# Modulation weights in pieces of 256 rows by 512 columns, loaded behind all of x, summed in operations of 1024 columns

## Chip, cores and metric

One core of a Trainium2 chip. The metric is the device time of one execution in microseconds (us), as the median of the runs shown. The engines are PE (TensorE: matrix products and transposes), DVE (VectorE), ACT (ScalarE), POOL (GpSimd) and SP (SyncE, which here only issues DMA transfers). They run in parallel, each in its own program order, and wait for one another by semaphores.

## The reference, cut to what the change touches

```python
def _rmsnorm(x, g):
    inv = lax.rsqrt(jnp.mean(x * x, axis=-1, keepdims=True) + EPS)
    return (x * inv) * g

def reference(x, c, w_ada, b_ada, norm_g, w_in, ...):
    mod = c @ w_ada[l] + b_ada[l]                      # 1024 -> 3 * 1024
    shift, scale, gate = jnp.split(mod, 3, axis=-1)
    h = _rmsnorm(x, norm_g[l]) * (1.0 + scale[:, None, :]) + shift[:, None, :]
    proj = h @ w_in[l]                                 # q, k, v, z of two attentions, gates
    ...                                                # attentions, gated merge, w_out, residual
    return _rmsnorm(x, final_g)
```

x is 1024 x 1024 in float32, c one row of 1024, w_ada 1024 x 3072. `shift` and `scale` are the first two thirds of `c @ w_ada`; the residual's `gate` is made later and is not touched.

## The kernel before

The program is one launch. The part that matters here is its start (`with tc.tile_pool(name="start")`, from L193), which takes x, normalises it, turns it so that the model's columns lie on the partitions, modulates it, and makes the first projections from it. The rest (further projections, two attentions, merge, output) follows and is the same text before and after.

x is held as eight tiles of 128 tokens, four in `xa` and two each in the two `xb`. The turned and normalised x is `xnT`, eight blocks k = 0 to 7 of 128 columns on the partitions by 1024 tokens. The steps of the start are functions, and the string `SEQ` (L44) sets in which order they are written, and with it the order on every engine. A word is a letter and a number: `X` loads a tile of x (L206), `L` a block of the modulation's weights (L213), `R` one of the first four blocks of w_in (L157; all three on the SP queue); `s` sums the squares of a tile on ACT (L238); `n` makes the 1/rms of four tiles, `inv`, on ACT and DVE (L245 to L247, then three small DVE steps in L188 to L190); `x` turns a tile, by scaling it on DVE (L257) and transposing it on PE (L266), or by a product with a scaled identity, `diag` (L255, L264), and copies it out of PSUM on DVE or ACT (L267).

`a` (`weigh`) forms `am`, the sum over q of c[q] times row block q of the weights, for shift and scale, with the partitions still apart: on DVE one product (L275) and seven multiply-adds onto it (L277, scalar_tensor_tensor). `f` (`factors`) sums `am` over the partitions by two small matmuls with ones into PSUM bank 1 of `pv`, which has one buffer (L288), and DVE reads them into `ashf` and `amul` (L290, L291); the next `f` waits for that reading. `m` (`modulate`) applies the two on ACT (L297) and splits the result into a high part `hhi` (a cast on ACT, L161) and a rest `hlo` (a subtraction on DVE, L162). `w` splits a block of w_in in the same way; for the four blocks of the start the subtraction runs on POOL (`POOLW`). `p` (`project`) makes three matmuls (L177 to L179) for each k and each of seven accumulators of 512 tokens: 7 x 8 x 3 = 168. The letters l and r are halves. Behind the last `p` the accumulators are evacuated (from L376) and the rest of the kernel begins.

Before, a weight block holds all 1024 rows of the columns of one k (two for k = 3 and 4): in `GROUPS` each is a block for itself, `ADATAG` names the buffer. A row of a block is 128 or 256 columns, 512 bytes or 1 KB. The first block is loaded between the first tile of x and the others.

Of the kernel before, what the change touches and what calls it, by code (L numbers as in the profile page):

```python
# [8 lines left out]
F32 = mybir.dt.float32  # L9
# [5 lines left out]
ALU = mybir.AluOpType  # L15
# [3 lines left out]
P = 128  # L19
S = 1024  # L20
D = 1024
HD = 64
KB = D // P
# [4 lines left out]
FCOL = 4096  # L28
GCOL = 4104
FP = 2  # L30
PEK = ()
EVACS = "k0 z0 g0 g1 q0 k1 q1"
PRE = 8
GACT = 1
# [4 lines left out]
POOLW = (0, 1, 2, 3)  # L39
BATCH = (4,)  # L40
CPY = "dd aa aa aa ad dd ad aa"
GROUPS = ((0,), (1,), (2,), (3, 4), (5,), (6,), (7,))
ADATAG = ("ada1", "ada1b", "ada1", "ada2", "xb1", "ada1b", "ada1")
SEQ = "X2 L0 X0 s0 X1 X3 X4 s3 a0 X7 s2 X6 X5 s1 n0 x0 L1 s4 s5 s7 s6 R0 L2 x2 f0 R2 L3 n1 x1 a3 a1 x3 x4 R1 w0 x5 f1 x7 x6 R3 m0l w1l L6 w1r m0r m1l m1r a2 w3l L5 w2 f2 a5 f3 m2 m3l a6 p0l p1l f4 p0r w3r p1r m3r f5 p2l L7 f6 m4 m5l p2r p3l p3r a7 f7 m6 m5r m7l p4 p5 p6l p6r m7r p7"  # L44
WPOOL = ()
MLAG = 2
GAHEAD = 1
# [21 lines left out]
def tile_hybrid_block(ctx, tc, x, c, w_ada, b_ada, norm_g, w_in, b_forget,  # L69
                      w_o_sb, w_o_fox, b_gate, w_out, final_g, out):  # L70
    nc = tc.nc
    x2 = x[0]
    out2 = out[0]
    wada = w_ada[0]
# [28 lines left out]
    def pv_tile(b=None):  # L103
        if b is None:
            b = bank2[0] = 1 - bank2[0]
        return ps_pv.tile([P, 512], F32, name="pv", tag="pv%d" % b)
# [6 lines left out]
    ones = const.tile([P, 1], F32, name="ones")  # L113
# [15 lines left out]
    cT = cols[:, 0:8]  # L129
# [63 lines left out]
    with tc.tile_pool(name="start", bufs=1) as sp:  # L193
# [2 lines left out]
        xt = [xa[:, t, :] for t in range(4)] + [xb[t // 2][:, t % 2, :] for t in range(4)]  # L196
        xnT = sp.tile([P, KB, S], F32, name="xnT")
        half = {"": slice(0, S), "l": slice(0, 512), "r": slice(512, S)}
        group = {k: g for g in GROUPS for k in g}
        edges = (0,) + BATCH + (TB,)  # L200
        batch = {t: b for b in range(len(edges) - 1) for t in range(edges[b], edges[b + 1])}
        adas, ams, raws, norms, sums, wsplit, bank = {}, {}, {}, {}, {}, {}, [0]
# [2 lines left out]
        def load_x(t):  # L205
            nc.sync.dma_start(xt[t], x2[t * P:(t + 1) * P, :])  # L206

        def load_ada(k):
            n = len(group[k]) * P
            tag = ADATAG[GROUPS.index(group[k])]  # L210
            ada = sp.tile([P, KB, 2, n], F32, name="ada", tag=tag, bufs=1)
            for j in range(2):
                nc.sync.dma_start(ada[:, :, j, :],  # L213
                                  wada[:, j * D + k * P: j * D + k * P + n].rearrange("(q p) n -> p q n", p=P))
            adas[k] = ada

        def load_w0(i):
            raws[i] = load_raw(wcol((QA, KA, GCOL + 8 * P, ZA)[i]), WSH)
# [47 lines left out]
                        nc.tensor.transpose(o, i, ident)  # L266
                copy(xnT[:, 4 * b:4 * b + 4, t * P:(t + 1) * P], pt.rearrange("p (a b) -> p a b", a=4))  # L267

        def weigh(k):

            n = len(group[k]) * P
            if k in PEK:
                return
            o = ams[k] = sp.tile([P, 2, n], F32, name="am", tag="am%d" % n, bufs=2)
            nc.vector.tensor_scalar(o, adas[k][:, 0], cT[:, 0:1], None, ALU.mult)  # L275
            for q in range(1, KB):
                nc.vector.scalar_tensor_tensor(o, adas[k][:, q], cT[:, q:q + 1], o, ALU.mult, ALU.add)  # L277

        def factors(k):
            k0 = group[k][0]  # L280
            pm = pv_tile(1)
            for j in range(2):
                if k in PEK:
                    for q in range(KB):
                        nc.tensor.matmul(pm[:, j:j + 1], adas[k][:, q, j, :], cT[:, q:q + 1], start=q == 0,
                                         stop=q == KB - 1)
                    continue
                nc.tensor.matmul(pm[:, j:j + 1], ams[k0][:, j, (k - k0) * P:(k - k0 + 1) * P], ones,  # L288
                                 start=True, stop=True)
            nc.vector.tensor_add(ashf[:, k:k + 1], pm[:, 0:1], b_shift[:, k:k + 1])  # L290
            nc.vector.scalar_tensor_tensor(amul[:, k:k + 1], pm[:, 1:2], b_scale1[:, k:k + 1], gT[:, k:k + 1],  # L291
                                           ALU.add, ALU.mult)
# [22 lines left out]
        def project(k, part):  # L315
            accumulators()
            for hf in {"": (0, 1), "l": (0,), "r": (1,)}[part]:
                for i in range(4):
                    if hf < len(accs[i]):
                        proj_mm(accs[i][hf], wsplit[i], hf, k, k == 0, k == KB - 1)  # L320

        todo = dict(X=load_x, L=load_ada, R=load_w0, s=square, n=norm, x=turn_x, a=weigh, f=factors, m=modulate,
                    w=split_w, p=project)
        for what in SEQ.split():
            todo[what[0]](int(what[1]), *([what[2:]] if what[0] in "mwp" else []))
# [133 lines left out]
    def largest(p):  # L459


        pt = tp_tile()
        nc.tensor.transpose(pt[0:1, :P], vmost[p], ident)
        top = at.tile([1, 1], F32, name="vtop", tag="vtop", bufs=2)
        nc.vector.tensor_reduce(top, pt[0:1, :P], mybir.AxisListType.X, ALU.max)
        nc.vector.tensor_scalar(top, top, 1e-25, None, ALU.max)
        e = top.bitcast(I32)
        nc.vector.tensor_scalar(e, e, 0x7F800000, None, ALU.bitwise_and)
        pair = vscale[p] = at.tile([1, 2], F32, name="vpow", tag="vpow", bufs=2)
        nc.vector.tensor_scalar(pair[:, 0:1].bitcast(I32), e, -1.0, float((254 + VSCALE) << 23), ALU.mult, ALU.add)  # L470
        nc.vector.tensor_scalar(pair[:, 1:2].bitcast(I32), e, 1.0, float((VSCALE + 15) << 23), ALU.mult, ALU.subtract)

    def spread(p):

        pt = tp_tile()
        nc.tensor.matmul(pt[:, 0:2], ones_row, vscale[p], start=True, stop=True)
        o = at.tile([P, 2], F32, name="vsc", tag="vsc", bufs=2)
        nc.vector.tensor_copy(o, pt[:, 0:2])
        for q in (p, p + 1):
            vscale[q], vback[q] = o[:, 0:1], o[:, 1:2]  # L480

    def sprinkle(units, marks):

        seen, marks = [0], list(marks)

        def wrap(gen):
            for _ in gen:
                seen[0] += 1
                while marks and marks[0][0] <= seen[0]:
                    marks.pop(0)[1]()  # L490
                yield 1
        for u in units:
            u.gen = wrap(u.gen)
        assert marks[-1][0] < sum(u.steps for u in units)
        return units
# [51 lines left out]
    def load_v(p):  # L547
        vraw[p] = load_raw(vd[p], [P, S], "vraw").rearrange("p (a b d) -> p a b d", a=TB, b=2)

    def take_v(p):  # L550
        raw = vraw[p]
        vv[p] = at.tile([P, TB, 2, P], F16, name="vv", tag="vv", bufs=2)
        hi, lo = vv[p][:, :, :, 0:HD], vv[p][:, :, :, HD:P]
        nc.scalar.activation(hi, raw, AF.Identity, scale=vscale[p])
        for b in range(2):
            nc.vector.scalar_tensor_tensor(lo[:, :, b], raw[:, :, b], vscale[p], hi[:, :, b], ALU.mult, ALU.subtract)
# [26 lines left out]
    def residual_gate():  # L583

        box, raw = [], {}

        def load(k):
            raw[k] = at.tile([P, D], F32, name="graw", tag="graw")
            nc.sync.dma_start(raw[k], wada[k * P:(k + 1) * P, 2 * D:3 * D])

        def weigh(k):
            if k == 0:
                box.append(at.tile([P, D], F32, name="gacc", tag="fb", bufs=2))
                box.append(at.tile([1, D], F32, name="grow", tag="fb", bufs=2))
                nc.sync.dma_start(box[1], b_ada[0:1, 2 * D:3 * D])
                nc.vector.tensor_scalar(box[0], raw[0], cT[:, 0:1], None, ALU.mult)
            else:
                nc.vector.scalar_tensor_tensor(box[0], raw[k], cT[:, k:k + 1], box[0], ALU.mult, ALU.add)

        def total(hf):  # L600
            acc, row = box
            t = slice(hf * 512, hf * 512 + 512)
            ps = tp_tile()
            nc.tensor.matmul(ps[:1], ones, acc[:, t], start=True, stop=True)
            nc.vector.tensor_add(row[:, t], ps[:1], row[:, t])
            if hf == 1:
                nc.sync.dma_start(gated, row)
        return [lambda f=f, k=k: f(k) for k in range(KB) for f in (load, weigh)] + \
               [lambda hf=hf: total(hf) for hf in range(2)]
# [411 lines left out]
    for p in range(7):  # L1021
        a, b = [], []
        if p == 0:
            g = sprinkle(gs.pop(0), [(3, lambda: largest(0)), (4, lambda: load_v(0)), (6, lambda: spread(0)),
                                     (9, lambda: take_v(0))])
# [12 lines left out]
        q = p + 1  # L1038
# [38 lines left out]
    for t in range(TB):  # L1077
# [12 lines left out]
        for i, (c0, c1) in enumerate(zip(cuts, cuts[1:])):  # L1090
            n = slice(c0, c1)
# [53 lines left out]
```

## Time and profile before

| | |
|---|---|
| median of 3 runs | 958.14 us (957.44 to 959.42) |
| the profiled execution's own time | 960.62 us |
| its span in the profile | 958.9 us |
| mean granted clock of PE | 0.983 |
| busy: PE, DVE, ACT, POOL | 901.8, 708.1, 601.9, 117.4 us |

The profile is one execution; its times are counted from the start of the span. PE's granted clock is a share of full speed: 1.00 is the level of 2.4 GHz, 0.50 that of 1.2 GHz. The start stage, to which the change is confined, lasts until about 82 us.

### The profile page before, as it was taken

The page shows a single profiled execution, that of the slowest core. Times are in us where ns is not written, and L with a number is a line of the kernel's source. Part 1 is how long each engine was busy: PE and PEld are TensorE (multiplying, and loading weights), DVE is VectorE, ACT ScalarE, POOL GpSimd, SP SyncE. Part 2 cuts the span into 40 slices and gives each one's busy share as a digit, 9 for nine tenths or more (in the row PEclk, how much of TensorE's full clock was granted, in tenths as well). Part 3 has the DMA queues.
Part 4 walks back from the last instruction along what each step waited for, and adds up shares of the span by engine and source line. Part 5 has one row for each costly group of instructions (what it writes and reads, how often), then busy time and mean ns, then how long its engine had stood idle before and what let it go on. Part 6 is the DMA issues. An engine that isn't in the chain of part 4 may idle for free.

```text
span 958.9 us, 14911 instructions
## 1 busy us (share of the span) xinstructions
PE 901.8 (94%) x5282; PEld 756.8 (79%) x5282; DVE 708.1 (74%) x1402; ACT 601.9 (63%) x1102; POOL 117.4 (12%) x191
## 2 busy tenths in 40 slices
PE   2899999999999999889999999999899998999997
PEld 2678878879878777668987888998787777788886
DVE  4984989687786788789787777657776767676544
ACT  5646777776677687678778776546656456543222
POOL 0401001000010000100001112211313011440000
PEclk9999999999999999989999999999999999899999
DMA  9943476635794562975567677958997998552221
GB/s 313 297 116 86 99 204 125 150 96 108 168 168 119 130 160 78 175 192 114 118 168 151 162 184 160 182 142 194 200 193 146 266 265 205 207 175 88 92 94 58
DMA packets 260655, 152.14 MB, mean 159 GB/s; under 512 B 157154, under 2 KB 241746, under 8 KB 260580
## 3 DMA queue, kind: packets, MB, share of 16 engines
q1 hardware_dynamic: 257588, 142.78, 60.5%
q0 software_dynamic: 2880, 8.39, 4.7%
q8 instruction: 41, 0.67, 0.3%
q14 instruction: 34, 0.28, 0.1%
q10 hardware_dynamic: 112, 0.02, 0.0%
HBM read 80.31 MB, written 24.71 MB: 110 GB/s over the span
## 4 chain that ended last, share of the span: by engine, by line
PE 45%; DVE 11%; DMA 6%; ACT 4%; issue 3%; POOL 0%; SPq 0%; DVEq 0%; ACTq 0%; POOLq 0%
PE acc L177 7%; PE acc L178 6%; PE acc L179 6%; PE z L179 4%; PE z L178 4%; PE z L177 4%; DVE pw L707 2%; DMA graw<-in_w_ada_dram 2%; PE pv L755 2%; DMA wT<-pc 2%; PE pv L756 2%; PE acc L526 2%; PE z L622 2%; PE acc L528 2%; PE z L624 2%
## 5 line engine op out<-in xcount | busy, mean ns | idle before, releaser
L177 PE MATMUL acc<-hhi,w 128*128 128x512 f32 x576 | 235.1, 408 | 13.0 <-DVE ks L377 5.4
L179 PE MATMUL acc<-hhi,w 128*128 128x512 f32 x576 | 227.6, 395 | 0.0
L178 PE MATMUL acc<-hlo,w 128*128 128x512 f32 x576 | 227.4, 395 | 0.0
L177 PEld LDWEIGHTS acc<-hhi,w 128*128 128x128 f32 x576 | 110.1, 191 | 37.2 <-issue 9.0
L725 DVE SCALAR_TENSOR_TENSOR pc<-pw,pc 128x1024 f16<-128x1024 f32 (+7 forms) x128 | 96.8, 759 | 43.3 <-ACT pc L721 42.9
L179 PEld LDWEIGHTS acc<-hhi,w 128*128 128x128 f32 x576 | 109.6, 190 | 24.1
L178 PEld LDWEIGHTS acc<-hlo,w 128*128 128x128 f32 x576 | 110.0, 191 | 19.3
L721 ACT ACTIVATE pc<-pw 128x1024 f16<-128x1024 f32 (+7 forms) x128 | 86.8, 680 | 16.3 <-DMA wT<-pc 14.7
L717 ACT ACTIVATE pw<-pw,low 128x1024 f32<-128x1024 f32 (+3 forms) x64 | 49.6, 774 | 63.0 <-DVE low L712 63.0
L765 POOL TENSOR_TENSOR ysb<-ysb,fac 128x128 f32<-128x128 f32 x64 | 34.9, 546 | 429.2 <-DVE ysb L764 283.5
L719 ACT ACTIVATE pw<-pw,low 128x1024 f32<-128x1024 f32 (+3 forms) x64 | 49.4, 772 | 47.9 <-DVE low L712 46.6
L755 PE MATMUL pv<-vv,wT 128*128 128x128 f16 x576 | 73.9, 223 | 1.7 <-DMA wT<-pc 1.7
L756 PE MATMUL pv<-vv,wT 128*128 128x128 f16 x576 | 73.7, 222 | 0.0
L526 PE MATMUL acc<-wv,hhi 128*128 128x256 f32 (+1 forms) x256 | 73.5, 287 | 0.0
L528 PE MATMUL acc<-wv,hlo 128*128 128x256 f32 (+1 forms) x256 | 72.4, 283 | 0.0
L527 PE MATMUL acc<-wv,hhi 128*128 128x256 f32 (+1 forms) x256 | 72.4, 283 | 0.0
L622 PE MATMUL z<-ks,qs 128*128 128x512 f32 (+1 forms) x192 | 66.7, 347 | 1.5 <-DVE yT L777 1.3
L700 DVE SCALAR_TENSOR_TENSOR pw<-z,pw 128x512 f32<-128x512 f32 (+4 forms) x96 | 52.8, 551 | 17.9 <-ACT pw L691 17.3
L624 PE MATMUL z<-kx,qs 128*128 128x512 f32 (+1 forms) x192 | 65.6, 342 | 0.0
L162 DVE TENSOR_TENSOR w<-wraw,w 128x1024 fp32r<-128x1024 f32 x44 | 54.0, 1228 | 12.5 <-ACT w L161 12.2
L755 PEld LDWEIGHTS <-wT 128*128 128x128 f16 x576 | 56.7, 100 | 6.9 <-issue 4.1
L707 DVE TENSOR_TENSOR_SCAN pw<-pw 128x512 f32<-128x512 f32 (+2 forms) x64 | 58.8, 919 | 1.0
(273 smaller groups left out, 2001.3 us busy)
## 6 DMA issues: line engine op xcount, KB each, us to landing
wraw<-in_w_in_dram SPq DMA_DIRECT2D x48, 512.0 KB, 5.9
gd<-stg SPq DMA_DIRECT2D x32, 256.0 KB, 3.0
kx<-ks POOLq DMA_DIRECT2D x28, 256.0 KB, 5.4
ada<-in_w_ada_dram SPq DMA_DIRECT2D x12, 512.0 KB, 8.0
graw<-in_w_ada_dram SPq DMA_DIRECT2D x8, 512.0 KB, 4.4
zd<-stg SPq DMA_DIRECT2D x16, 256.0 KB, 4.0
zt<-zd SPq DMA_DIRECT2D x32, 128.0 KB, 2.8
vraw<-vd SPq DMA_DIRECT2D x8, 512.0 KB, 3.5
```

Of the source, the lines that this page charges most:

```text
L177: nc.tensor.matmul(ps, w[0], x[0], start=first, stop=False)
L178: nc.tensor.matmul(ps, w[0], x[1], start=False, stop=False)
L179: nc.tensor.matmul(ps, w[1], x[0], start=False, stop=last)
L526: nc.tensor.matmul(ps[:, a], hhi[k][:, t], hi[:, k, :], start=k == 0, stop=False)
L528: nc.tensor.matmul(ps[:, a], hlo[k][:, t], hi[:, k, :], start=False, stop=k == KB - 1)
L622: nc.tensor.matmul(o, qs[p, j][:, tq], ks[p, j][:, s], start=True, stop=False)
L624: nc.tensor.matmul(o, qs[p, j][:, tq], kx[p, j][:, s], start=False, stop=not mask)
L707: nc.vector.tensor_tensor_scan(l[:, ::-1], l[:, ::-1], l[:, ::-1], carry[0], ALU.add, ALU.bypass)
L721: nc.scalar.activation(pair.parts(a)[0], w, AF.Copy, scale=WSCALE)
L725: nc.vector.scalar_tensor_tensor(lo, pair.logits(a), WSCALE, hi, ALU.mult, ALU.subtract)
L755: nc.tensor.matmul(y[:, a, :], w[:, b + s, :], v, start=s == 0, stop=False)
L756: nc.tensor.matmul(y[:, a, :], w[:, b + nb + s, :], v, start=False, stop=s == nb - 1)
```

## The change

The weights of shift and scale are cut otherwise. A load is now a piece of 256 rows (two row blocks q) and 512 columns (four k), for shift and for scale: 1 MB in two transfers, in runs of 2 KB. There are eight pieces, 0 to 3 for k = 0 to 3 and 4 to 7 for k = 4 to 7, in three buffers. All eight tiles of x are loaded ahead of the first piece. `weigh` of a piece makes two operations, one for each q, of 2 x 512 = 1024 columns; after four pieces `am` is whole for four k. So `factors` of k = 0 to 3 all stand behind the fourth piece, and those of k = 4 to 7 behind the eighth. `SEQ` is written anew for that. `PEK`, `GROUPS` and `ADATAG` go.

```diff
-GROUPS = ((0,), (1,), (2,), (3, 4), (5,), (6,), (7,))
-ADATAG = ("ada1", "ada1b", "ada1", "ada2", "xb1", "ada1b", "ada1")
-SEQ = "X2 L0 X0 s0 X1 X3 X4 s3 a0 X7 s2 X6 X5 s1 n0 x0 L1 s4 s5 s7 s6 R0 L2 x2 f0 R2 L3 n1 x1 a3 a1 x3 x4 R1 w0 x5 f1 x7 x6 R3 m0l w1l L6 w1r m0r m1l m1r a2 w3l L5 w2 f2 a5 f3 m2 m3l a6 p0l p1l f4 p0r w3r p1r m3r f5 p2l L7 f6 m4 m5l p2r p3l p3r a7 f7 m6 m5r m7l p4 p5 p6l p6r m7r p7"
+SEQ = "X2 X0 s0 X1 X3 X4 s3 X7 s2 X6 X5 s1 L0 L1 n0 x0 L2 s4 s5 s7 s6 a0 x2 L3 R0 n1 x1 a1 x3 x4 R1 a2 L4 w0 x5 x7 x6 a3 R2 L5 f0 m0l w1l f1 w1r m0r m1l m1r f2 R3 a4 L6 w2 f3 m2 m3l w3l p0l p1l a5 L7 p0r w3r p1r m3r p2l a6 a7 f4 f5 p2r p3l p3r f6 f7 m4 m5l m6 m5r m7l p4 p5 p6l p6r m7r p7"
...
-        def load_ada(k):
-            n = len(group[k]) * P
-            tag = ADATAG[GROUPS.index(group[k])]
-            ada = sp.tile([P, KB, 2, n], F32, name="ada", tag=tag, bufs=1)
+        def load_ada(i):
+
+            ada = adas[i] = sp.tile([P, 2, 2, 512], F32, name="ada", tag="ada", bufs=3)
+            rows_ = wada[i % 4 * 2 * P:(i % 4 + 1) * 2 * P, :]
             for j in range(2):
-                nc.sync.dma_start(ada[:, :, j, :],
-                                  wada[:, j * D + k * P: j * D + k * P + n].rearrange("(q p) n -> p q n", p=P))
-            adas[k] = ada
+                c0 = j * D + i // 4 * 512
+                nc.sync.dma_start(ada[:, :, j, :], rows_[:, c0:c0 + 512].rearrange("(q p) n -> p q n", p=P))
...
-        def weigh(k):
-
-            n = len(group[k]) * P
-            if k in PEK:
-                return
-            o = ams[k] = sp.tile([P, 2, n], F32, name="am", tag="am%d" % n, bufs=2)
-            nc.vector.tensor_scalar(o, adas[k][:, 0], cT[:, 0:1], None, ALU.mult)
-            for q in range(1, KB):
-                nc.vector.scalar_tensor_tensor(o, adas[k][:, q], cT[:, q:q + 1], o, ALU.mult, ALU.add)
+        def weigh(i):
+
+            g = i // 4
+            if i % 4 == 0:
+                ams[g] = sp.tile([P, 2, 512], F32, name="am", tag="am", bufs=2)
+            for x in range(2):
+                q = i % 4 * 2 + x
+                if q == 0:
+                    nc.vector.tensor_scalar(ams[g], adas[i][:, x], cT[:, 0:1], None, ALU.mult)
+                else:
+                    nc.vector.scalar_tensor_tensor(ams[g], adas[i][:, x], cT[:, q:q + 1], ams[g], ALU.mult, ALU.add)
...
-                nc.tensor.matmul(pm[:, j:j + 1], ams[k0][:, j, (k - k0) * P:(k - k0 + 1) * P], ones,
+                nc.tensor.matmul(pm[:, j:j + 1], ams[k // 4][:, j, k % 4 * P:(k % 4 + 1) * P], ones,
                                  start=True, stop=True)
```

How this moves instructions is shown at three places. Line numbers of the changed kernel are 2 to 3 lower than before around `load_ada` and 7 lower behind `factors`; so L274, L276 are its product and multiply-add, L281 its factors' matmul, L175 to L177 its projection.

The first place is the SP queue at the start of the program, `xa` and `xb` being x, `ada` the modulation's weights and `wraw` w_in. Before:

```order
L206 DMA xa<-in_x_dram 128x1024
L213 DMA ada<-in_w_ada_dram 128x8x128 x2
L206 DMA xa<-in_x_dram 128x1024 x3
L206 DMA xb_169<-in_x_dram 128x1024
L206 DMA xb_170<-in_x_dram 128x1024 x2
L206 DMA xb_169<-in_x_dram 128x1024
L213 DMA ada<-in_w_ada_dram 128x8x128 x2
L157 DMA wraw<-in_w_in_dram 128x8x128
```

The same queue in the changed kernel:

```order
L204 DMA xa<-in_x_dram 128x1024 x4
L204 DMA xb_169<-in_x_dram 128x1024
L204 DMA xb_170<-in_x_dram 128x1024 x2
L204 DMA xb_169<-in_x_dram 128x1024
L212 DMA ada<-in_w_ada_dram 128x2x512 x8
L155 DMA wraw<-in_w_in_dram 128x8x128 x2
```

The first block of weights has moved from the second place to behind all of x, and four pieces now stand ahead of the first block of w_in.

The second place is DVE from the scaling of the second half of x to the first `hlo`. Before:

```order
L255 TENSOR_SCALAR diag<-ident,inv 128x128
L257 TENSOR_SCALAR xb_169<-xb_169,inv 128x1024
L290 TENSOR_TENSOR ashf<-pv,cols 128x1
L291 SCALAR_TENSOR_TENSOR amul<-pv,b_scale_132,cols 128x1
L257 TENSOR_SCALAR xb_170<-xb_170,inv 128x1024
L255 TENSOR_SCALAR diag<-ident,inv 128x128
L275 TENSOR_SCALAR am<-ada,cols 128x256
L267 COPY xnT<-tp 128x4x128
L267 COPY xnT<-acc 128x4x128
L267 COPY xnT<-z 128x4x128
L162 TENSOR_TENSOR hlo<-xnT,hhi 128x512
```

In the changed kernel, from the scaling of the second `xb` (L254) to the first of four pairs that read factors (L283, L284):

```order
L254 TENSOR_SCALAR xb_170<-xb_170,inv 128x1024
L276 SCALAR_TENSOR_TENSOR am<-ada,cols,am 128x1024
L264 COPY xnT<-tp 128x4x128
L276 SCALAR_TENSOR_TENSOR am<-ada,cols,am 128x1024
L264 COPY xnT<-acc 128x4x128
L276 SCALAR_TENSOR_TENSOR am<-ada,cols,am 128x1024
L264 COPY xnT<-z 128x4x128
L252 TENSOR_SCALAR diag<-ident,inv 128x128
L276 SCALAR_TENSOR_TENSOR am<-ada,cols,am 128x1024 x2
L264 COPY xnT<-tp 128x4x128
L283 TENSOR_TENSOR ashf<-pv,cols 128x1
L284 SCALAR_TENSOR_TENSOR amul<-pv,b_scale_132,cols 128x1
```

The long weight operations now stand between the copies, and no factor is read until the last of them.

The third place is PE at the first projections; `z`, `tp` and `acc` are PSUM banks, `wqk` and `wz` split blocks of w_in. Before:

```order
L266 MATMUL tp<-ident,xb_170 128x128 x4
L177 MATMUL z<-hhi,wqk 128x512
L266 MATMUL acc<-ident,xb_170 128x128 x4
L177 MATMUL acc<-hhi,wz 128x512
L264 MATMUL z<-diag,xb_170 128x128 x4
L264 MATMUL tp<-diag,xb_170 128x128 x4
L178 MATMUL z<-hlo,wqk 128x512
```

In the changed kernel:

```order
L263 MATMUL tp<-ident,xb_170 128x128 x4
L263 MATMUL acc<-ident,xb_170 128x128 x4
L261 MATMUL z<-diag,xb_170 128x128 x4
L261 MATMUL tp<-diag,xb_170 128x128 x4
L281 MATMUL pv<-ones,am 128x1 x8
L175 MATMUL z<-hhi,wqk 128x512 x3
L175 MATMUL tp<-hhi,wqk 128x512
```

The projections no longer stand among the last transposes; the factors' eight small matmuls (four k) stand between the two.

## Rows read from the trace of the kernel before

**Rows 1.** Page, section 1: busy us (share of the span) xinstructions.
```profile
PE 901.8 (94%) x5282; PEld 756.8 (79%) x5282; DVE 708.1 (74%) x1402; ACT 601.9 (63%) x1102; POOL 117.4 (12%) x191
```

**Rows 2.** Timeline, PE and ACT: start, us, engine line op out<-in [idle before <-releaser].
```profile
31.76 0.48 PE L177 MATMUL z<-hhi,wqk 128*128 128x512 f32 x1
...
49.66 0.61 PE L288 MATMUL pv<-ones,am 128*128 128x1 f32 x4 [1.01 <-DVE am L277]
...
81.32 0.39 PE L179 MATMUL acc<-hhi,wz 128*128 128x512 f32 x1
81.55 0.39 PE L177 MATMUL pv<-hhi,w 128*128 128x512 f32 x1
...
81.12 0.58 ACT L376 CAST ks<-z 64x512 fp32r<-64x512 f32 x1 [6.14 <-PE tp L179]
```

**Rows 3.** Windows, PE alone: from:to length, busy (x), granted clock, DMA share, GB/s.
```profile
52.00:55.40 3.40, 3.40 (x9) 0.50 0.59 147
55.40:81.50 26.10, 26.10 (x122) 1.00 0.16 42
```

**Rows 4.** Windows, busy of PE, PEld, DVE, ACT, POOL, then clock, DMA share, GB/s.
```profile
8.60:15.00 6.40, 1.09 (x5) 0.93 (x4) 4.42 (x14) 3.83 (x7) 0.00 (x0) 1.00 1.03 410
17.00:26.00 9.00, 7.34 (x40) 7.29 (x40) 7.46 (x21) 6.38 (x16) 0.00 (x0) 1.00 1.18 291
28.20:31.80 3.60, 2.09 (x20) 1.85 (x19) 3.60 (x4) 3.01 (x5) 2.66 (x2) 1.00 1.09 348
```

**Rows 5.** Timeline, DVE, from the first `inv` to the copies of x.
```profile
17.65 0.16 DVE L190 SCALAR_TENSOR_TENSOR inv<-nwt,inv 128x4 f32<-128x4 f32 x1
...
25.80 0.16 DVE L190 SCALAR_TENSOR_TENSOR inv<-nwt,inv 128x4 f32<-128x4 f32 x1
...
26.32 0.28 DVE L255 TENSOR_SCALAR diag<-ident,inv 128x128 f32<-128x128 f32 x1
...
28.03 2.40 DVE L255 TENSOR_SCALAR diag<-ident,inv 128x128 f32<-128x128 f32 x1
...
31.21 0.67 DVE L267 COPY xnT<-acc 128x512 f32<-128x512 f32 x1
```

**Rows 6.** Groups by line and shape, DVE, 0 to 95: busy us, mean ns.
```profile
L277 DVE SCALAR_TENSOR_TENSOR am<-ada,cols,am 128x256 f32<-128x256 f32 x42 | 19.3, 480 | 0.5
L277 DVE SCALAR_TENSOR_TENSOR am<-ada,cols,am 128x512 f32<-128x512 f32 x7 | 6.7, 957 | 0.1
L257 DVE TENSOR_SCALAR xa<-xa,inv 128x1024 f32<-128x1024 f32 x3 | 2.2, 751 | 0.0
```

**Rows 7.** Timeline, DVE, weight operations and `hlo` of two widths.
```profile
44.24 2.32 DVE L277 SCALAR_TENSOR_TENSOR am<-ada,cols,am 128x512 f32<-128x512 f32 x3
...
46.60 3.01 DVE L277 SCALAR_TENSOR_TENSOR am<-ada,cols,am 128x512 f32<-128x512 f32 x2
49.52 1.22 DVE L162 TENSOR_TENSOR hlo<-xnT,hhi 128x1024 fp32r<-128x1024 f32 x1
...
53.04 0.69 DVE L162 TENSOR_TENSOR hlo<-xnT,hhi 128x512 fp32r<-128x512 f32 x1
```

**Rows 8.** Timeline, POOL: three of the splits of w_in.
```profile
27.94 2.40 POOL L162 TENSOR_TENSOR wqk<-wraw,wqk 128x1024 fp32r<-128x1024 f32 x1 [26.22 <-ACT wqk L161]
31.28 2.38 POOL L162 TENSOR_TENSOR wz<-wraw,wz 128x1024 fp32r<-128x1024 f32 x1 [0.94 <-DVE xnT L267]
...
46.40 1.86 POOL L162 TENSOR_TENSOR w<-wraw,w 128x768 fp32r<-128x768 f32 x1 [4.80 <-ACT w L161]
```

**Rows 9.** Timeline, ACT: the squares of the last tile of x to arrive.
```profile
17.45 1.06 ACT L238 ACTIVATE sq<-xb 128x1024 bf16<-128x1024 f32 x1 [0.22 <-DMA xb<-in_x_dram]
```

**Rows 10.** Timeline, PE and DVE: one factor's matmuls and their reading.
```profile
51.38 0.50 PE L288 MATMUL pv<-ones,am 128*128 128x1 f32 x4
...
51.92 0.16 DVE L290 TENSOR_TENSOR ashf<-pv,cols 128x1 f32<-128x1 f32 x1 [0.99 <-PE pv L288]
51.99 0.21 DVE L291 SCALAR_TENSOR_TENSOR amul<-pv,b_scale,cols 128x1 f32<-128x1 f32 x1
```

More of the change, by code (lines that the diff above doesn't have):

```diff
@@ L30 @@
 FP = 2
-PEK = ()
 EVACS = "k0 z0 g0 g1 q0 k1 q1"
@@ L198, in tile_hybrid_block @@
         half = {"": slice(0, S), "l": slice(0, 512), "r": slice(512, S)}
-        group = {k: g for g in GROUPS for k in g}
         edges = (0,) + BATCH + (TB,)
@@ L267, in turn_x @@
                 copy(xnT[:, 4 * b:4 * b + 4, t * P:(t + 1) * P], pt.rearrange("p (a b) -> p a b", a=4))
-        def weigh(k):
-            n = len(group[k]) * P
-            if k in PEK:
-                return
-            o = ams[k] = sp.tile([P, 2, n], F32, name="am", tag="am%d" % n, bufs=2)
-            nc.vector.tensor_scalar(o, adas[k][:, 0], cT[:, 0:1], None, ALU.mult)
-            for q in range(1, KB):
-                nc.vector.scalar_tensor_tensor(o, adas[k][:, q], cT[:, q:q + 1], o, ALU.mult, ALU.add)
+        def weigh(i):
[8 more added lines that the diff above has]
+                    nc.vector.scalar_tensor_tensor(ams[g], adas[i][:, x], cT[:, q:q + 1], ams[g], ALU.mult, ALU.add)
         def factors(k):
-            k0 = group[k][0]
             pm = pv_tile(1)
             for j in range(2):
[L283 to L287, printed above, removed]
-                nc.tensor.matmul(pm[:, j:j + 1], ams[k0][:, j, (k - k0) * P:(k - k0 + 1) * P], ones,
+                nc.tensor.matmul(pm[:, j:j + 1], ams[k // 4][:, j, k % 4 * P:(k % 4 + 1) * P], ones,
                                  start=True, stop=True)
```

## The prediction

> **What bounds the kernel now.** The page was read first: TensorE (PE) is busy for 901.8 of 958.9 us, 94% [rows 1]. That is an average over stages, and the change lies in the start stage alone, so the next views were the timelines of the engines up to 85 us. (The page's chain is given as shares and names no place in the start, so it does not decide here.) The projections of the start begin at 31.76, and the last of their 168 matmuls of 512 columns issues at 81.32 [rows 2]. ScalarE (ACT), which evacuates them, had then waited 6.14 us for PE [rows 2]. So the end of the start is where PE's projections end, and the rest of the kernel shifts with it.
>
> Two stretches make up that time. Up to 49.66 PE waits, again and again, for VectorE (DVE): the factors' matmuls at 49.66 had waited 1.01 us for the weighted sum `am` [rows 2]. After 49.66 PE runs without a gap, at a granted clock of 0.50 from 52.0 to 55.4 and of 1.00 afterwards [rows 3]. In the full-clock stretch one such matmul issues every 0.227 us (two neighbours at the end, 81.32 and 81.55 [rows 2]), in the slow one every 0.425 us (the window's nine records in 3.40 us, the first and last of them in part). So the reader is to look for the moment from which PE has no more to wait for; before it, DVE's list is the bound, after it PE's count of matmuls.
>
> **The change, term by term.** Times are from the start of the profiled span.
>
> A. *x before the weights.* Before, the first weight block (1.05 MB in 512-byte runs) lies between the first tile of x and the others. It goes behind them. x itself moves at 410 GB/s, 512-byte runs at 291, 1 KB runs at 348 [rows 4]. The block's removal is worth 1.05/0.410 = 2.6 us to 1.05/0.291 = 3.6 us; I take 3.6, since these are its own runs. The first `inv`, ready at 17.8 [rows 5], then stands at 14.2. The second, ready at 26.0 [rows 5], has two weight operations (0.48 busy each [rows 6]) put between its last three steps; without them these steps wait for one another instead, which I put at 0.6 us saved, so it stands at 26.0 - 3.6 - 0.6 = 21.8.
>
> The Trainium skill (DMA: Bandwidth & Descriptors, Specifications) says that transfers of 512 bytes and more reach line rate. The measured 291 against 410 GB/s does not agree with it. By the rule the term would be 2.6, not 3.6.
>
> B. *DVE's list to the first `am`.* The 49 scalar_tensor_tensor of before take 19.3 + 6.7 = 26.0 us [rows 6]. After, there are 14, of 1024 columns, a shape that the trace of before does not show. Three of 512 columns, each on the result of the one before, take 2.32 us [rows 7]: 0.75 for the last and 0.787 from start to start ahead of it. 512 more columns cost 1.22 - 0.69 = 0.53 by the two sizes of `hlo` [rows 7], so one takes 1.28, 1.32 apart in a chain and about 1.20 with something else between. Bounds: 0.957 x 2 = 1.91, the mean of the 512-column form with POOL's disturbance in it [rows 6], and 1.06, twice the extra 0.53 with nothing fixed. 14 x 1.28 is 17.9, so 8 us of DVE leave. But they no longer come one block at a time: all of k = 0 to 3 must be summed before the first factor. From 21.8 there are: 2 `diag` 2 x 0.2 = 0.4 (0.28 busy), 2 scalings of x 2 x 0.67 = 1.3 (0.75 busy [rows 6]), 3 copies from PSUM 3 x 0.6 = 1.8 (0.67 busy; each starts 0.08 before the one ahead is done [rows 5]), 6 weight operations 5 x 1.20 + 1.32 = 7.3, and one split of a w_in block on POOL (GpSimd), which holds DVE up for its 2.4 us. That is 13.2, so `am` is ready at 35.0.
>
> The hold-up is read from a pair of rows. A `diag`, 0.28 at 26.32, lasts 2.40 at 28.03, while POOL's split runs from 27.94 to 30.34 [rows 5, 8]. Two weight operations from 46.60 take 3.01 instead of 1.54 beside POOL's 1.86 from 46.40 [rows 7, 8]. A copy from PSUM, at 31.21, takes its 0.67 beside POOL's next one [rows 5, 8]. So operations that read SBUF alone lose 80 to 90% of a POOL split, and copies from PSUM nothing.
>
> The transfers don't set this. All of x and the first block had landed by 17.4, when the last square of x had waited for its tile [rows 9]; without the block that is about 14. Four pieces of 1.05 MB in 2 KB runs, at a speed between those of 1 KB and 4 KB runs, take 11 us (25 us); at 291 GB/s they would take 14.4 (28.4). The last piece's first operation comes up at about 30.1. The new wait of the SP queue, where the fourth piece waits for the buffer of the first (three buffers), holds the two w_in loads queued behind it as well; the first piece is summed by about 20 (14.2 and 5.5 of DVE's list), so the queue issues the fourth while the third is still on its way. That costs nothing unless the cover of 1.7 to 5 us goes.
>
> C. *Four factors in a row.* All four pairs of small matmuls stand ahead of the first projection, share one PSUM bank, and each waits for DVE's reading of the one before. From the start of a pair to the end of its `amul` is 51.38 to 52.20 = 0.82 us [rows 10]; with the way back to PE I take 1.0. Bounds are 0.82 and 1.72, from 49.66 to 51.38 with other work between [rows 2, 10]. Modulation and cast of the first block pass beside it on ACT. First projection: 35.0 + 3 x 1.0 + 0.5 = 38.5, against 31.76 [rows 2]. DVE is free at 39.0. Before, PE spent this stretch on transposes with projections among them; now these stand apart.
>
> D. *DVE's list to the second `am`.* One first product 0.67, six `hlo` of 512 columns 6 x 0.6 = 3.6, one of 1024 columns 1.1, seven weight operations 8.7, and POOL's splits 2.4 + 0.6 + 1.8 = 4.8 (from 2.38 for 1024 columns, 1.86 for 768, and a quarter of 2.38 for 256 [rows 8]; the second block's pieces run beside the factors): 18.9. The second `am` is ready at 57.9. In the meantime PE issues 65 matmuls, 14.7 us, in 19.4 us, so it waits 4.7 us for `hlo` and `am`.
>
> E. *PE to the end.* 103 of 168 matmuls are left at 57.9: 23.3 us, and four factors' pairs of 0.45: 1.8. The end is 83.0 against 81.55: +1.5 us. This uses POOL's splits at full length, 7.2 us in B and D; at 85% it is 1.1 less, so +0.4. I take +1.0, between the two.
>
> So a gain of 3.6 and 8 us on engines that wait comes to nothing, because the first projection starts 7 us later and PE's later idle time, which hid that, is used up. Sum: profiled execution 960.6 + 1.0 = 961.6 (span 958.9, and 1.7 around it), and by the median of the runs, which lies 2.5 lower, **958.14 + 1.0 = 959.1 us**.
>
> **Rivals.** All times are from the median.
>
> 1. *Faster: POOL's splits don't hold the longer operations up.* Then 2.4 leaves B and 4.8 D. First projection at 36.1; the second `am` is ready at 50.7, before PE needs it; PE then needs 168 x 0.227 + 1.8 = 39.9 from 36.1, with 1 us of waits 77.0, or -4.5: 953.6 us. For it: a copy beside POOL lost nothing. Against it: the weight operation from 46.60 is of the same kind and did lose time [rows 7, 8]. Chance 0.17.
>
> 2. *Slower: PE's clock falls behind the second `am`.* Before, it fell to 0.50 (the 1.2 GHz level) at 52.0, after PE had waited 1.01 us before 49.66, and stayed for eight matmuls, 8 x (0.425 - 0.227) = 1.6 us [rows 2, 3]. My sum has no fall, and PE waits more often before 57.9. It decides from 57.9 on, where PE has no idle time to absorb it; a fall earlier costs nothing. 960.7 us; two, 962.3. Against it: it was one stretch of 3.4 us in 50. Chance 0.25. The Trainium skill (TensorE: Matmul & The Clock Gate, HAM oscillation — how this bites in real kernels) describes the same: PE waits for data, is throttled again, and the next work starts cold. The trace's fall behind the waits for `am` agrees in kind.
>
> 3. *Slower: the first pieces come too late.* If the four pieces land behind 30.1, B is set by SP's queue: at 230 GB/s they would end at 14 + 18.2 = 32.2 and cost 2 us, 961.2. It decides below 260 GB/s; the windows of before with a full queue show 291 or more [rows 4]. Chance 0.06.
>
> 4. *The line-rate rule of 512 bytes.* x gains 2.6, not 3.6, everything comes 1 us later: 960.1. Chance 0.05; the measured 291 speaks against it (the page is named at A).
>
> **How the numbers follow.** A measurement of this kernel can tell about 0.2%, 1.9 us: the bounds are 956.2 and 960.1. The forecast has 0.47, of which 0.03 lies over 960.1 (POOL's splits and the factors at their upper bounds), 0.44 in between. Faster: rival 1, 0.17. Slower: 0.25 + 0.06 + 0.05 + 0.03 = 0.39. Together 1.00. The forecast's own range is 957.5 (factors at 0.82, -0.7, and POOL at 80%, -1.4, from the full sum at 959.6) to 960.4 (POOL in full, factors at 1.2, +0.8). The range to be given reaches to 956.0, where half of POOL's time holds nothing up (-3.5 from the full sum at 959.6), and to 962.6, two falls; outside lie most of rival 1 and a little of 3.
>
> **What would show it.** In the changed kernel's trace: 14 weight operations of about 1.28 us, two or three of them lengthened beside POOL's splits; `inv` ready at 14.2 and 21.8; the first four factors from 35.0; first projection at 38.5; second batch of factors from about 57.9; last matmul of the start at 83.0; and the granted clock by stretch. If the first projection comes before 36.5 with no lengthened operation, rival 1 holds. If the fourth piece lands after 30, rival 3. If PE still waits after 60, the list in D is too short or something else (`hlo`, a factor) is late. The prediction is wrong altogether if the rest of the kernel does not shift with the start's end, for example because a transfer or a cast queued behind the start moves by another amount.

## The result and the profile after

| | before | changed |
|---|---|---|
| median of 14 runs each | 956.12 us (954.55 to 960.07) | 961.29 us (956.77 to 965.54) |
| ratio | | 1.0053, 95% interval 1.0039 to 1.0068 |
| profiled execution, its span | 960.62, 958.9 us | 960.05, 958.3 us |

The changed kernel is slower by 5.1 us (3.7 to 6.5). That lies inside the range on record but is not "the same" (956.2 to 960.1), which was given the largest chance, and it is five times the forecast +1.0. The base moved too: the first three runs of before had a median of 958.14, all 14 have 956.12. Counted from the 958.14 that the forecast started from, the range was -2.1 to +4.5 us, and +5.1 lies above that. So it is luck that 961.29 lies inside the range. And the two profiled executions say the opposite of the runs: the changed one is 0.6 us shorter. A ratio below is not the quotient of the two medians beside it, and it leaves out single runs that were more than 1.5% above their kernel's fastest, so the two can differ by up to about 1 us. So the first question is not what the change did, but which of these numbers to believe.

The start in the changed kernel's trace, first DVE (start, us, operation; [idle before <- what ended it]); L188 makes `inv`, L274 and L276 are the weights' product and multiply-adds:

```profile
14.15 0.17 DVE L188 SCALAR_TENSOR_TENSOR inv<-nwt,inv 128x4 f32<-128x4 f32 x1
...
21.33 0.17 DVE L188 SCALAR_TENSOR_TENSOR inv<-nwt,inv 128x4 f32<-128x4 f32 x1
...
27.85 1.28 DVE L276 SCALAR_TENSOR_TENSOR am<-ada,cols,am 128x1024 f32<-128x1024 f32 x1
...
29.83 4.58 DVE L276 SCALAR_TENSOR_TENSOR am<-ada,cols,am 128x1024 f32<-128x1024 f32 x2
...
43.14 5.12 DVE L276 SCALAR_TENSOR_TENSOR am<-ada,cols,am 128x1024 f32<-128x1024 f32 x2
```

Then PE (L281 are the factors, L175 to L177 the projections) and, last, ACT's first evacuation:

```profile
34.47 0.61 PE L281 MATMUL pv<-ones,am 128*128 128x1 f32 x4 [0.89 <-DVE am L276]
35.45 0.61 PE L281 MATMUL pv<-ones,am 128*128 128x1 f32 x4 [0.37 <-DVE amul L284]
36.43 0.81 PE L281 MATMUL pv<-ones,am 128*128 128x1 f32 x4 [0.38 <-DVE amul L284]
37.62 1.02 PE L281 MATMUL pv<-ones,am 128*128 128x1 f32 x4 [0.38 <-DVE amul L284]
38.50 1.63 PE L175 MATMUL z<-hhi,wqk 128*128 128x512 f32 x3
...
57.34 0.61 PE L281 MATMUL pv<-ones,am 128*128 128x1 f32 x4 [0.95 <-DVE am L276]
...
82.45 0.39 PE L177 MATMUL acc<-hhi,wz 128*128 128x512 f32 x1
...
82.25 0.58 ACT L369 CAST ks<-z 64x512 fp32r<-64x512 f32 x1 [13.51 <-PE tp L177]
```

Against [rows 2]: the first projection comes at 38.50 instead of 31.76, the last at 82.45 instead of 81.32, ACT's first evacuation at 82.25 instead of 81.12. By this pair of traces the start costs +1.1 us, as forecast. PE's windows of the changed kernel (length, busy (x), granted clock, DMA share, GB/s) show the clock:

```profile
29.80:33.30 3.50, 3.33 (x15) 0.51 1.10 340
33.30:36.70 3.40, 1.76 (x14) 1.00 1.07 363
36.70:43.60 6.90, 6.52 (x20) 0.51 0.67 199
43.60:57.30 13.70, 12.59 (x55) 1.00 0.63 187
57.30:82.40 25.10, 25.06 (x118) 1.00 0.17 44
```

10 us at the 1.2 GHz level, against 3.4 in before [rows 3], but all of it ahead of 57.34, where PE then waits 0.95 us for `am` all the same. DVE, whose list makes that `am`, was busy for 18.2 of the 18.3 us from 38.9 to 57.2, so PE's low clock did not hold it up there; ahead of that it shows only in the last factors, 1.19 us apart instead of 0.98. In before the one slow stretch lies behind the last wait, at 52.0 to 55.4, where it delays everything. The reader is to keep that difference in mind; the experiments turn on it.

### The profile page after: what moved, and what is told of

The parts are those of the page before. It is cut to its first block, busy times and chain, and to the rows that moved or that the text cites. A ratio compares the mean times of both kernels' runs of the same rounds, so it can differ in the third digit from the quotient of the medians.

```text
span 958.3 us, 14877 instructions
## 1 busy us (share of the span) xinstructions
PE 896.6 (94%) x5282; PEld 753.1 (79%) x5282; DVE 701.5 (73%) x1362; ACT 600.8 (63%) x1102; POOL 124.0 (13%) x191
## 5 line engine op out<-in xcount | busy, mean ns | idle before, releaser
L175 PE MATMUL acc<-hhi,w 128*128 128x512 f32 x576 | 233.8, 406 | 14.5 <-DVE ks L370 5.9
L177 PE MATMUL acc<-hhi,w 128*128 128x512 f32 x576 | 226.3, 393 | 0.0
L175 PEld LDWEIGHTS acc<-hhi,w 128*128 128x128 f32 x576 | 109.5, 190 | 38.2 <-issue 7.2
L177 PEld LDWEIGHTS acc<-hhi,w 128*128 128x128 f32 x576 | 108.9, 189 | 23.8
L714 ACT ACTIVATE pc<-pw 128x1024 f16<-128x1024 f32 (+7 forms) x128 | 86.8, 680 | 15.9 <-DMA wT<-pc 14.2
L748 PE MATMUL pv<-vv,wT 128*128 128x128 f16 x576 | 72.2, 220 | 2.2 <-DMA wT<-pc 2.2
L749 PE MATMUL pv<-vv,wT 128*128 128x128 f16 x576 | 72.0, 219 | 0.0
L693 DVE SCALAR_TENSOR_TENSOR pw<-z,pw 128x512 f32<-128x512 f32 (+4 forms) x96 | 52.9, 552 | 18.3 <-ACT pw L684 16.8
```

The costliest lines, as they stand in the source:

```text
L175: nc.tensor.matmul(ps, w[0], x[0], start=first, stop=False)
L177: nc.tensor.matmul(ps, w[1], x[0], start=False, stop=last)
L714: nc.scalar.activation(pair.parts(a)[0], w, AF.Copy, scale=WSCALE)
L748: nc.tensor.matmul(y[:, a, :], w[:, b + s, :], v, start=s == 0, stop=False)
L749: nc.tensor.matmul(y[:, a, :], w[:, b + nb + s, :], v, start=False, stop=s == nb - 1)
```

## The experiments

**Each kernel once more.** No edit.

> The kernel before once more, against itself, as a second trace of it and a measure of how far two medians of one kernel lie apart. All theories: ratio 1.000 within 0.002, start's last projection matmul (the pv bank's L179) within 1 us of the first trace. Theory S (the start alone): stretches of granted clock 0.50 lie elsewhere than in the first trace and account for most of the difference in span between the two traces. Theory L (something later than the start): the stretches behind the start take the same time in both traces once the slow-clock stretches are taken off.

> The changed kernel once more. Theory S: only the start is longer, by the 1.1 us that the two traces show (last projection matmul about 1.1 us later), and the rest of the measured 5 us came from slow-clock stretches that fell more often in these runs by chance; then the ratio here is 1.001 to 1.003 (+1 to +3 us). Theory L: the loss of 5 us is a property of the kernel, the ratio is again 1.004 to 1.007, and a trace taken here is 3 us or more longer behind 85 us than a trace of before in the same stretches.

Before against itself: 1.0005 (0.9990 to 1.0020). The changed kernel again: 960.34 against 955.36, 1.0059 (1.0041 to 1.0078). So the loss of 5 us came again, and the first pair of traces was misleading. The second trace of before, span 955.3, shows how (PE's windows in the first fence, ACT's first evacuation in the second):

```profile
43.80:47.20 3.40, 3.40 (x10) 0.50 0.99 271
47.20:79.50 32.30, 32.30 (x153) 1.00 0.34 90
```

```profile
79.31 0.58 ACT L376 CAST ks<-z 64x512 fp32r<-64x512 f32 x1 [6.13 <-PE tp L179]
```

Here the slow stretch fell at 43.8 to 47.2, 8 us earlier than in [rows 3], into the part where PE waits for DVE anyway (1.01 us at 49.66 in the first trace; in the second that wait is gone). The start ended 1.8 us earlier, at 79.31, where I had expected the two within 1 us. The changed kernel's second trace ended its start at 82.00, as the first did at 82.25. So the start costs +1.1 us against one trace of before and +2.7 to +2.9 against the other. Behind the start, the changed kernel took 876.0 and 874.8 us in its two traces, before 877.8 and 876.0: no loss there in these four. But the four are not typical of their kernels' runs: both of before took longer than its median (960.62 and 956.98 us), both of the changed kernel less than its own (960.05 and 959.59).

**The start alone.** Behind `SEQ` the accumulators are copied out and the rest is left out; the second kernel below is the changed start, the third has one part of the change (next experiment):

```diff
             todo[what[0]](int(what[1]), *([what[2:]] if what[0] in "mwp" else []))
+        for i, b in enumerate(accs[0] + accs[1] + accs[2] + accs[3]):
+            (nc.vector.tensor_copy if i % 2 else nc.scalar.copy)(xnT[:, i, 0:512], b)
+        for k in range(KB):
+            nc.sync.dma_start(out2[k * P:(k + 1) * P, :], xnT[:, k, :])
+        return
```

> The start of the kernel before alone: behind its last projection the seven accumulators are copied to SBUF and written out, and everything that follows is left out (the output is not the reference's, and the two v blocks of w_in that the full kernel casts in this stretch are not there). Over several runs this shows what the start costs, and how much it varies with where the slow-clock stretch falls. Theory S: the start ends at 79.3 in most runs (slow stretch near 44, as in the second trace) and at 81.1 in some (at 52, as in the first); runs spread over about 2 us. Theory L: it ends near 81 in most runs.

> The start of the changed kernel alone, cut off in the same way (output not the reference's). Theory S (the loss is in the start and is hidden in the first pair of traces by where the slow stretch fell): median 2.5 to 5 us over the start of before. Theory L: median 1 to 2 us over it, the rest of the 5 us arises later. Both: less spread than before's start, since the slow stretches lie ahead of the second am, where PE waits anyway.

> The start alone (output not the reference's) of before with the first weight block behind all of x. In its full trace the slow stretches were 30.1 to 40.3 and 47.2 to 50.6 and the start ended 2.5 to 4.3 us later than in the two traces of before. Theory S: 3 to 5 us over the start of before. Theory L: 0 to 2 us.

Medians: before 89.98 us (88.77 to 90.56), changed 93.15 (92.45 to 95.06), x first 93.63 (92.66 to 94.30). By the ratios to the full kernel before, 0.0934 and 0.0973, the distance is 3.7 us, by the medians 3.2. The trace of before's start ends at 79.3 with its slow stretch at 44.2. So in the start alone the change costs 3.2 to 3.7 of the 5.1 us. In the traces of the whole kernels the start's end differs by 0.9 to 2.9 us (82.00 and 82.25 against 79.31 and 81.12), so its share of the whole kernel's loss is not settled closer than that. The base of my sum, 81.55, is of one kind of run: five traces have before's start (two of before, the two shifted kernels below, the start alone), and the slow stretch is at 52 in two of them and near 44 in three.

I had expected less spread in the changed start than in before's, and there is more, 2.6 against 1.8 us. Its trace is of the slowest of its runs, 95.06 us, and has a slow stretch behind the second `am`, whose factors stand at 57.94 (two of PE's matmuls in the stretch, and the last projection):

```profile
59.94 0.63 PE L177 MATMUL z<-hhi,wqk 128*128 128x512 f32 x1
60.37 0.63 PE L175 MATMUL acc<-hhi,wz 128*128 128x512 f32 x1
...
84.81 0.39 PE L177 MATMUL acc<-hhi,wz 128*128 128x512 f32 x1
```

From 59.3 to 62.7 the matmuls follow one another every 0.43 us, at a granted clock of 0.52, and the last projection is at 84.81 instead of 82.45. About 1.6 of these 2.4 us are the stretch, 0.6 the later `am`. So a slow stretch can fall on the path in the changed kernel too.

**One part alone: x first.** Before's blocks, widths and order, with the first block behind all of x (the beginning of `SEQ`):

```diff
-X2 L0 X0 s0 X1 X3 X4 s3 a0 X7 s2 X6 X5 s1 n0 x0 L1 s4
+X2 X0 s0 X1 X3 X4 s3 X7 s2 X6 X5 s1 L0 n0 x0 L1 a0 s4
```

> The kernel before with one part of the change alone: the first weight block is loaded behind all of x and summed after the first tile of x is turned; blocks, widths and the later order are as before. By term A of the prediction both inv come about 3.5 us earlier (ready at 14.3 and 22.5), the first projection about 1 to 3 us earlier than 31.8, and the start ends 0 to 2 us earlier, since DVE's list up to 49.6 has the same work in it. Theory S: time -0 to -2 us. Theory L, if the loss comes from x ahead of the weights (DMA order, later loads): +2 us or more although the start ends no later.

961.77 against 955.36, 1.0068 (1.0047 to 1.0089): x first alone costs 6.4 us, as much as the whole change or more, where I had expected a gain of up to 2. In the start alone it is 3.65 by the medians. Its trace (PE's windows in the first fence; PE's longest wait and ACT's first evacuation in the second):

```profile
30.10:40.30 10.20, 7.89 (x32) 0.50 1.14 315
47.20:50.60 3.40, 3.40 (x9) 0.50 0.88 245
```

```profile
31.84 1.12 PE L266 MATMUL tp<-ident,xb 128*128 128x128 f32 x4 [4.21 <-DVE xnT L267]
...
83.58 0.58 ACT L376 CAST ks<-z 64x512 fp32r<-64x512 f32 x1 [6.13 <-PE tp L179]
```

Before, DVE forms the first `am` while it has nothing else to do, waiting for x, whose first `inv` comes at 17.65 [rows 5]:

```profile
9.49 3.61 DVE L277 SCALAR_TENSOR_TENSOR am<-ada,cols,am 128x256 f32<-128x256 f32 x7
```

With x first those 4 us of weight operations go behind the first `inv`, into the list that PE waits for (4.21 us at 31.84). The first projection comes earlier, at 27.16, but the 3.6 us that x gains are lost again. The clock, which did not fall before 43 in any trace of before, is at 0.50 from 30.1 to 40.3, and in that stretch DVE in its turn waits for PE:

```profile
34.92 0.16 DVE L290 TENSOR_TENSOR ashf<-pv,cols 128x1 f32<-128x1 f32 x1 [1.15 <-PE pv L288]
...
39.27 0.69 DVE L267 COPY xnT<-tp 128x512 f32<-128x512 f32 x1 [1.45 <-PE tp L264]
```

In before's trace DVE has no wait from 27.0 to 43.4. So the longer list and the low clock both take part in the loss, and no run separates them. From 47.2 the clock is at 0.50 once more, behind PE's last longer wait, which delays the end.

**The other part alone: wide pieces, weights early.** The changed start with piece 0 where before has its first block (the beginning of its `SEQ`):

```diff
-X2 X0 s0 X1 X3 X4 s3 X7 s2 X6 X5 s1 L0 L1 n0 x0 L2 s4 s5 s7 s6 a0 x2 L3
+X2 L0 X0 s0 X1 X3 X4 s3 a0 X7 s2 X6 X5 s1 L1 n0 x0 L2 s4 s5 s7 s6 x2 L3
```

> The start alone (output not the reference's) of the changed kernel with its first piece of weights loaded where before has its first block, between the first tile of x and the others, and summed before x is turned: the wide pieces without x ahead of them. By the prediction's sums x and both inv come 3.5 us later than in the changed kernel, and two weight operations of 1.9 us leave DVE's list behind the first inv: first factors 1.5 us later, start 94.5 us. If the early idle time of DVE is worth more than that, or PE's clock stays up because PE waits less, 91 to 93 us.

92.42 us (92.07 to 92.71). It was to be 1.5 slower than the changed start and is 0.7 faster by the medians, 0.5 by the ratios to before (0.0968 against 0.0973, with intervals that overlap). The first factors did come later by about as much as forecast (35.66 against 34.47), the second `am` did not (its factors at 56.87 against 57.34). So inside the wide scheme too, an early piece costs nothing against an early x; that it is worth more is not shown. But the start is still 2.4 over before's 89.98 (3.2 by the ratios): the wide pieces, with the order that goes with them, cost that by themselves. I read it from the traces as the price of holding the first factor back until all four k are summed and the fifth until all eight are; no run changes that alone. The parts don't add up (3.65 and 2.4 alone, 3.2 together). That both use up the same waiting time of PE would explain it, and is not tested.

**POOL's splits.** The changed kernel with `POOLW = ()`, so that the four subtractions run on DVE.

> The changed kernel with the four splits of w_in taken from POOL and put on DVE (POOLW empty). If POOL's splits hold DVE up as the prediction's terms B and D have it (in the changed trace 2.0 us beside 29.8, 2.5 beside 43.1, 1.6 beside 48.2, 6.1 in all), DVE pays 4 x 1.13 = 4.5 us for them itself and gets 6.1 back: the second am comes about 1.6 us earlier than 57.3, and the time falls by 1 to 2 us against the changed kernel (960.3 to 959). If POOL's splits cost DVE nothing (rival 1), the second am comes 4.5 us later and the time rises by 4 to 5 us.

The two groups of weight operations (busy us, mean ns of one), first with the splits on POOL, then with them on DVE:

```profile
L276 DVE SCALAR_TENSOR_TENSOR am<-ada,cols,am 128x1024 f32<-128x1024 f32 x14 | 22.4, 1602 | 0.2
```

```profile
L276 DVE SCALAR_TENSOR_TENSOR am<-ada,cols,am 128x1024 f32<-128x1024 f32 x14 | 17.9, 1281 | 0.1
```

The second batch of factors on PE, in the kernel with the splits on DVE:

```profile
57.75 0.50 PE L281 MATMUL pv<-ones,am 128*128 128x1 f32 x4
```

With no split on POOL the fourteen take 1.281 us each, as term B had it (1.28), and 4.5 us less in all. So POOL does hold them up, and rival 1 falls. The second batch of factors is at 57.75 against 57.34, the start ends at 82.64 against 82.25: moving the splits to DVE costs it about what POOL took from it. I had expected 1.6 us back. The time was 963.11, 1.0074 (1.0057 to 1.0092), by the ratios 1.4 to 2.0 us over the changed kernel (1.0059 and 1.0053), where I had expected 1 to 2 less. The intervals overlap, the start in this trace explains 0.4, and the rest is open.

**The clock.** The changed kernel with 21 bf16 matmuls that nobody reads in PE's idle time from 24 to 38, each as

```diff
+                nc.tensor.matmul(pm, ident16, sqs[-1][:, 0:512], start=True, stop=True)
```

> The changed kernel with 21 small-cost bf16 matmuls of 512 columns (0.23 us each at full clock, into a bank that nobody reads) in PE's idle time between 24 and 38 us, where it waits for DVE's long weight operations and the factors; every other instruction in the same order. If the waiting is what brings the clock down to 0.50 at 29 to 33 and 36 to 43 us, the slow stretches there go. Theory DVE (the second am sets the end of the start): start and time fall by 1 us at most, 960. Theory clock (the slow stretches are the loss): -2 to -4 us, 957 to 958.

> The start alone of the same (output not the reference's, as in the other kernels of the start alone). Theory DVE: 92 to 93 us, against 93.0 of the changed start. Theory clock: 89 to 91.

961.66 us, 1.0074 (1.0048 to 1.0101); the start alone 93.50 (93.13 to 94.50). PE's windows, and in the second fence the start's end:

```profile
29.00:37.20 8.20, 4.81 (x32) 1.00 1.08 343
37.20:44.00 6.80, 6.31 (x18) 0.50 0.53 164
```

```profile
82.13 0.58 ACT L380 CAST ks<-z 64x512 fp32r<-64x512 f32 x1 [13.51 <-PE tp L177]
```

The slow stretch at 30 to 33 is gone from this trace, the one from 37 is not: 6.8 of 10 us remain. In the trace of the start alone nothing is gained, it is at 0.50 from 34.9 to 45.0. The added matmuls also delay the factors and with them the first projection, from 38.50 to 40.47. And yet the second factors come at 57.28 (57.34 without them), and the end of the start is where it was, 82.13. So in these traces of the changed kernel neither PE's first projection nor the early slow stretch sets the start's end; the second `am` does, and 103 matmuls behind it. Theory clock did not bring the gain that it named, in the start or in the whole. But as a test of it this is a weak one, since most of the slow time remained.

**A pure shift.** Before, with five and with fourteen matmuls more ahead of the last k's projections, where PE has no idle time (shown for five):

```diff
         def project(k, part):
             accumulators()
+            if k == KB - 1:
+                pm = pv_tile(1)
+                for j in range(5):
+                    nc.tensor.matmul(pm, wsplit[0][0][:, 0, :], hhi[0][:, 0:512], start=True, stop=True)
```

> The kernel before with five more matmuls of 512 columns (into a bank that nobody reads) ahead of the projections of the last k, where PE has no idle time: the start ends 5 x 0.227 = 1.1 us later, as in the changed kernel, and nothing else is changed. Theory S: +1.1 us. Theory L in the form that a later end of the start is enough to disturb what follows (a transfer or a cast that no longer fits): +3 to +6 us, as the changed kernel. If the changed kernel is again 5 us slower and this one only 1, the later loss is tied to something else in the change than the shift.

> The kernel before with fourteen more matmuls of 512 columns (into a bank that nobody reads) ahead of the projections of the last k: the start ends 14 x 0.227 = 3.2 us later, as much as the start alone of the changed kernel took more than that of before (93.0 against 89.9). If the rest of the kernel only shifts: +3.2 us, and the 2 us that the changed kernel lost beyond that are tied to something else in it or are chance. If any shift of the rest brings slow-clock stretches (five matmuls gave +2.9 instead of 1.1): +5 us or more, with a mean granted clock near 0.982 to 0.985 instead of 0.988.

Five: 958.22 against 955.36, 1.0028 (1.0012 to 1.0044), +2.7 us for a shift of 1.1. Fourteen: 959.69 against 955.23, 1.0059 (1.0036 to 1.0082), +4.5 by the medians and +5.6 by the ratio for a shift of 3.2. Both lie 1.3 to 2.4 above the shift, and both intervals reach down to about the shift itself (1.1 and 3.4). So the 1.4 to 1.9 us by which the changed kernel's loss exceeds its start's may need no cause of its own: delaying the start by matmuls alone does about the same. What causes it remains open. The mean granted clock of the runs points to slow stretches behind the start: 0.9874 to 0.9880 for before in these groups of runs, 0.9857 and 0.9863 for the two shifted kernels, 0.982 for the changed one; each 0.001 is about 1 us of PE's 900 us of work, an estimate. For the changed kernel 0.005 are 5 us, of which the start's 10.2 us of slow clock instead of 3.4 are 3.4 and hidden; 1.6 remain behind it. But in the single traces the slow time behind the start is 27 and 14 us in the two of before, 10 and 17 in the two of the changed kernel, so this is an argument from means, not shown place by place.

## Why the prediction was right and wrong

Term by term the sum held, to within 0.6 us:

| step | forecast | trace of the changed kernel |
|---|---|---|
| A: `inv` ready | 14.2, 21.8 | 14.3, 21.5 |
| B: first factors' matmuls | 35.0 | 34.47 |
| C: factors apart; first projection | 1.0; 38.5 | 0.98, 0.98, 1.19; 38.50 |
| D: second `am` read | 57.9 | 57.34 |
| E: end of the projections | 83.0 against 81.55: +1.5, with +1.0 taken | 82.45 against 81.32: +1.1 |

The unknown cost in B, a weight operation of 1024 columns, came out at 1.281 undisturbed. The two beside 29.83 took 4.58 instead of 2.6, as the rows of before had shown it for narrower ones [rows 5, 7, 8].

**The step that failed is the base in E.** I set the changed start's end against 81.55, the end in one trace of before, and that trace held a slow stretch of 3.4 us, worth 1.6, behind PE's last wait [rows 3]. I had priced exactly this stretch, in rival 2, and treated it as something that might be added to the changed kernel; in truth it was already in what I subtracted from. In the other trace of before, and in its start alone, the stretch lies near 44, in PE's waiting time, and the start ends at 79.3 to 79.5. Against that, the same sum gives 82.5 - 79.5 = +3.0, close to the 3.2 to 3.7 that the starts alone showed. There was a sign of it in the numbers I had: the profiled execution was 2.5 us above the median of its own runs. I carried the difference over from the one to the other unchanged.

**A second step, that the rest shifts one to one, is likely to be wrong too.** Two kernels that only shift it by 1.1 and 3.2 us lost 2.7 and 4.5, with intervals that reach down to about the shift. I had named this as what would make the prediction wrong, but gave it no size. A slip in the range: its upper end, 962.6, is called two falls of the clock, which rival 2 prices at 962.3.

The rivals: 1 (POOL holds nothing up) is refuted by the pair of groups above. 2 was right in its mechanism and priced right at 1.6, but I looked for it on one side only. In the first trace of before it was in the base already. In the changed kernel's two whole traces the start's slow stretches lie ahead of 57.3 and cost next to nothing; in the slowest run of its start alone one lies at 59.3, as rival 2 has it. How often each happens is not shown. 3 fell too: the first piece made DVE wait 0.51 us at 18.37, later ones not at all. 4 as a rule of the time fell with A: `inv` came 3.5 us earlier, as the 512-byte price gives, not 2.6. The Trainium skill (DMA: Bandwidth & Descriptors, Specifications) gives 512 bytes as the least transfer for line rate; the window of the changed kernel in which mostly 2 KB runs move shows 389 GB/s, against 291 and 348 for 512 bytes and 1 KB [rows 4], so the measured rate rises well beyond that size:

```profile
13.50:20.00 6.50, 4.85 (x25) 4.85 (x26) 5.59 (x11) 4.50 (x11) 0.00 (x0) 1.00 1.04 389
```

So the transfers did get faster and DVE's sums shorter, as the change intends: 22.4 us of multiply-adds instead of 26.0 in the two traces, and 8 us less by the undisturbed price. Neither was what the start waits for. In the first trace of before PE has no more to wait for behind 49.66; in the changed kernel it waits until 57.34. I put that down to two things, that DVE's early idle time is left unused and that no factor is there before four k are complete. The experiments show that each part of the change costs time by itself, not how the loss divides.

## What to carry to other kernels

Before a difference is added to a profiled execution, look for events in that execution that other runs need not share (here a slow-clock stretch on the path), and take a second trace or the program cut down to the stage before deciding by 1 us. Faster transfers and fewer operations in a stage are worth only what they move of the moment from which the bounding engine no longer waits; a block loaded early so that an idle engine can start on it can be worth more than the bytes that it delays. A wider operation delivers its first result later: ask who waits for the first, not for all.

## What the runs showed of the hardware

PE's granted clock was at 0.50 for 3.4 us in before's start, for 3.5 and 6.9 us in the changed kernel's and for 10.2 us with x first, and the same program has such stretches in different places from run to run: in before's start at 52.0 or near 44, behind it 27 us of slow clock in one trace and 14 in another. The two traces of before differ by 1.8 us in the start's end and by 3.6 us in their spans. How much of the spread of one kernel's runs, from 952.5 to 959.9 us in one group of 22, comes from that is not shown: the slowest of the 22 had a mean granted clock of 0.987, the mean of the group is 0.988.

DVE and POOL hold each other up in both directions. With the weight operations beside them, POOL's split of 1024 columns took 3.98 us instead of 2.38 [rows 8] in the changed kernel:

```profile
41.51 3.98 POOL L160 TENSOR_TENSOR wz<-wraw,wz 128x1024 fp32r<-128x1024 f32 x1 [4.74 <-ACT wz L159]
```

The Trainium skill (SBUF — State Buffer, SBUF: two separate sides) describes it as a lock on a port pair that one of the two holds for a whole instruction while the other stops. The rows agree: two weight operations lost 2.0 us beside the splits at 30.3, and with no split on POOL all fourteen ran at 1.28 us.
